# Five adaLN tiles from the mixer's output product to its first input products, conv LayerNorm steps scheduled earlier, conv chunks begun at once

## The chip, the cores and the metric

The kernel runs on one core of one Trainium2 chip. The metric is the device time of one execution in microseconds (us), the median of several runs. The core's engines run in parallel, each through its own instruction list in order: TensorE (PE, the matrix products), VectorE (DVE), ScalarE (ACT), GpSimd (POOL), and SyncE (SP), whose list here holds the DMA transfers.

## The reference

One block of a transformer on 256 tokens of width 2048, in float32. A conditioning vector is multiplied by a matrix (`w_ada`) and gives nine rows of shifts, scales and gates (adaLN). Then come a SwiGLU feed-forward (half weight), a mixer, and a second feed-forward, each with an RMS norm and a modulation before it and a gate after it. The mixer, which matters here:

```python
proj = jnp.einsum('bsd,de->bse', h, w_in)              # 2048 -> 5120 columns
q, k, v, conv_a, conv_g = jnp.split(proj, ...)
q = apply_rope(rms_norm(q, q_norm), cos, sin); k = apply_rope(rms_norm(k, k_norm), cos, sin)
attn = diff_attention(q, k, v, lam)                    # causal, two softmaxes, their difference
attn = (rms_norm(attn, subln) * (1.0 - lam_init)).reshape(B, S, ATTN_WIDTH)   # 1024 columns
u = conv_a * jax.nn.sigmoid(conv_g)                    # 1024 channels
u = causal_depthwise_conv(u, conv_w, conv_b)           # 31 taps along the tokens
u = jax.nn.silu(layer_norm(u, conv_ln_g, conv_ln_b))   # over the 1024 channels
merged = jnp.concatenate([attn, u], axis=-1)
return jnp.einsum('bse,ed->bsd', merged, w_out)        # 2048 -> 2048
```

## The kernel before

**Products.** float32 operands are split into a high part and a low part, and each product is three matmuls: high by high (L315), high of the activation by low of the weight (L316), low of the activation by high of the weight (L317), each 128x512. A weight tile is 128x2048 numbers (1 MB), fetched by SP into one of four `raw` buffers (`w_tile`). It is split in two halves: ACT makes `whi` (L294), DVE makes `wlo` (L296); each has four buffers, so two tiles are in flight. PE spends 24 matmuls on a tile, both 128-token tiles `t` included. Where a tile is held back or is the first of a stage, its halves lie in the general buffers and are called `blk`.

**adaLN.** `w_ada` is 144 further tiles of 1 MB. `ada(j)` fetches one into the same `raw` buffers (L180) and reduces it with the conditioning vector on DVE (L181, and a short read of the sum); each second one adds a bias (L185), and L223 makes a scale when a modulation is first asked for. `ada_share(r, limit)` lets a stage do r of these tiles on average until `limit` of them are done. They are spread over the stages that have room; 104 have to be there when the mixer ends.

**Mixer.** `w_in` is done in 10 chunks of 512 columns, `ci`, each with four weight tiles `pc`. Chunks 0 to 3 hold conv_a and conv_g (256 channels each), 4 to 9 are q, k, q, k, v, v. The first HOLD=3 chunks do their tile pc=0 together, while the norm's pieces still arrive (L425 to L430 are these pieces' modulation). After each tile's matmuls, work that was put off is called: `after_tiles(n, fn)` runs fn after n of the product's later steps, `tick` counts them. A finished chunk's results go into `pend`; they are taken up by `finish_mix` when the next chunk's first product has been issued. For chunks 0 to 3 that is `conv_chunk`: sigmoid and product (L777, L779), a transpose on PE and a copy (L788), the first of 31 taps by ACT (L769), and 60 taps on DVE (L771) put into the queue `bg`. `fill(n)` takes n taps from it after each tile; the table TAPS has n for each chunk.

**Output.** `w_out` has 16 tiles in order of `pc`, with n = 0, 1, 2 for each (12 tiles `i`), then n = 3 apart. pc = 0 and 1 need the attention half, pc = 2 and 3 the conv half (`mh[2]`, `mh[3]`). The first two tiles take TAPS_OUT taps; at i = 2 what is left of them is drained and `conv_ln` begins, in four steps: sums over channels (L937, L939, L941), mean by matmuls (L946), spreading over the partitions (L955), difference (L968) and squares, the sums again, the power on GpSimd (L977, L978), L955 once more, then scaling (L984), SiLU (L987) and the split into high (L990) and low (L991). Each step asks for the next by `after_tiles(1, ...)`.

**What sets the order.** Each instruction gets a priority in the order of the program's text; a scheduler writes each engine's list from priorities and dependencies before the run, and waits between the lists are semaphores. `tc.high_priority(offset=n)` moves what is written in its block n steps forward in that priority.

Of the kernel before, what the change touches and what calls it, by code (L numbers as in the profile page):

```python
# [35 lines left out]
UNITS = 3  # L36
PRE = 3
DVE_COLS = 2
AHEAD = 3
EXT = (1,) * 8 + (2,) * 4 + (3,) * 3  # L40
LOADS = [(0,), (1,), (2, 3), (4, 5), (6, 7)] + [(c,) for c in range(8, NCH)]
# [5 lines left out]
DUE = ((19, 8), (55, 16), (107, 24), (150, 32))  # L47


TAPS = (6, 6, 6, 6, 6, 6, 8, 6, 6, 6)  # L50
TAPS_OUT = 14
RMS_EPS = 1e-6
LN_EPS = 1e-5
LAM_INIT = 0.8 - 0.6 * float(np.exp(-0.3 * 0))
# [20 lines left out]
def block_kernel(ctx: ExitStack, tc: tile.TileContext, x_in, pos_in, w_ada, small, w_gu1, w_dn1,  # L75
# [56 lines left out]
    for i in range(4):  # L132
        pc = acc_tile()
# [13 lines left out]
    def fill(n):  # L147
        while n > 0 and bg:
            bg.popleft()()
            n -= 1  # L150

    def drain():
        while bg:
            bg.popleft()()
# [4 lines left out]
    def after_tiles(n, fn):  # L159
        later.append([n, fn])  # L160
# [116 lines left out]
    def w_tile(src, held=False, ks=(0, 4), small_raw=False):  # L277

        k0, n = ks[0], ks[1] - ks[0]
        src = src.rearrange("p (k n) -> p k n", k=4)  # L280
        if not small_raw:
            raw = rawp.tile([P, 4, 512], F32, tag="raw", name=nm("raw"))
            w_dma[0] = nc.sync.dma_start(out=raw[:, :n, :], in_=src[:, k0:k0 + n, :])
        views = {}
        for h in range(0, n, 2):
            m = min(2, n - h)
            if small_raw:
                part = blk([P, 2, 512])
                w_dma[0] = nc.sync.dma_start(out=part[:, :m, :], in_=src[:, k0 + h:k0 + h + m, :])
                rw = part[:, :m, :]  # L290
            else:
                rw = raw[:, h:h + m, :]
            hi = blk([P, 2, 512], F32R) if held else whp.tile([P, 2, 512], F32R, tag="whi", name=nm("whi"))
            nc.scalar.copy(out=hi[:, :m, :], in_=rw)  # L294
            lo = blk([P, 2, 512], F32R) if held else wlp.tile([P, 2, 512], F32R, tag="wlo", name=nm("wlo"))
            nc.vector.tensor_sub(out=lo[:, :m, :], in0=rw, in1=hi[:, :m, :].bitcast(F32))  # L296
            for j in range(m):
                views[k0 + h + j] = (hi[:, j, :], lo[:, j, :])
        return lambda j: views[j]
# [473 lines left out]
    def conv_chunk(cc, accs):  # L773
        us = []
        for t in range(NT):
            sg = tmp([P, 256])
            nc.scalar.activation(out=sg, in_=accs[t][:, 256:], func=AF.Sigmoid)  # L777
            u = tmp([P, 256])
            nc.vector.tensor_mul(out=u, in0=accs[t][:, :256], in1=sg)  # L779
            us.append(u)  # L780

        def rest():
            tp = tp_tile((P, 2, S))
            for t in range(NT):
                for i in range(2):
                    nc.tensor.transpose(tp[:, i, t * P:(t + 1) * P], us[t][:, i * P:(i + 1) * P], ident)
            uT[cc] = blk([P, 2, S])
            nc.scalar.copy(out=uT[cc], in_=tp)  # L788
            for j in reversed(range(CK)):
                for i in range(2):  # L790
                    bg.append(lambda i=i, j=j: conv_tap(cc, i, j))

        after_tiles(1, rest)
# [135 lines left out]
    def conv_ln():  # L929
        ones = tmp([P, 1])  # L930
        nc.gpsimd.memset(ones, 1.0 / 1024.0)

        def channel_mean(src):


            s4 = blk([P, 4, S])
            nc.vector.tensor_add(out=s4, in0=src[0], in1=src[1])  # L937
            s2 = tmp([P, 2, S])
            nc.vector.tensor_add(out=s2, in0=s4[:, :2, :], in1=s4[:, 2:, :])  # L939
            s1 = tmp([P, S])  # L940
            nc.vector.tensor_add(out=s1, in0=s2[:, 0, :], in1=s2[:, 1, :])  # L941

            def mean():
                m = tp_tile((P, NT))
                for t in range(NT):
                    nc.tensor.matmul(m[:, t:t + 1], s1[:, t * P:(t + 1) * P], ones, start=True, stop=True)  # L946
                return m

            return mean

        def spread(v):

            r = tp_tile((P, S))
            for t in range(NT):
                nc.tensor.transpose(r[:, t * P:(t + 1) * P], v[:, t:t + 1].to_broadcast([P, P]), ident)  # L955
            return r

        def stage1():
            summed = channel_mean(ytile)
            after_tiles(1, lambda: stage2(summed))  # L960

        def stage2(summed):
            mv = sm([P, NT], "rv")
            nc.vector.tensor_copy(out=mv, in_=summed())
            mean = spread(mv)
            sqs = []
            for b in range(2):
                nc.vector.tensor_sub(out=ytile[b], in0=ytile[b], in1=mean.unsqueeze(1).to_broadcast([P, 4, S]))  # L968
                q = blk([P, 4, S])
                nc.scalar.activation(out=q, in_=ytile[b], func=AF.Square)  # L970
                sqs.append(q)
            summed = channel_mean(sqs)
            after_tiles(1, lambda: stage3(summed))

        def stage3(summed):
            rv = sm([P, NT], "rv")
            nc.vector.tensor_scalar(out=rv, in0=summed(), scalar1=LN_EPS, scalar2=None, op0=ALU.add)  # L977
            nc.gpsimd.tensor_tensor(out=rv, in0=rv, in1=half[:, :NT], op=ALU.pow)  # L978
            after_tiles(1, lambda: stage4(rv))

        def stage4(rv):
            rs = spread(rv)
            for b in range(2):
                nc.vector.tensor_mul(out=ytile[b], in0=ytile[b], in1=rs.unsqueeze(1).to_broadcast([P, 4, S]))  # L984
                g0, b0 = _COLS["lng"][0] + 4 * b, _COLS["lnb"][0] + 4 * b
                for i in range(4):
                    nc.scalar.activation(out=ytile[b][:, i, :], in_=ytile[b][:, i, :], func=AF.Silu,  # L987
                                         scale=cst[:, g0 + i:g0 + i + 1], bias=cst[:, b0 + i:b0 + i + 1])
                mh[2 + b], ml[2 + b] = blk([P, 4, S], F32R), blk([P, 4, S], F32R)
                nc.scalar.copy(out=mh[2 + b], in_=ytile[b])  # L990
                nc.vector.tensor_sub(out=ml[2 + b], in0=ytile[b], in1=mh[2 + b].bitcast(F32))  # L991
                m_parts[2 + b] = NT

        stage1()


    kinds = [("q", 0), ("k", 0), ("q", 1), ("k", 1), ("v", 0), ("v", 1)]
    probs, avq = deque(), deque()

    def finish_mix(ci, accs):  # L1000
        if ci < 4:
            conv_chunk(ci, accs)
            return
        kind, g = kinds[ci - 4]
        if kind == "v":
            v_chunk(g, accs)
            avq.extend((g, qb, h_) for qb in range(2) for h_ in range(4))
        else:
            qk_chunk(kind, g, accs)
            if kind == "k":  # L1010
                if g == 0:
                    nc.scalar.activation(out=lsum, in_=lsum, func=AF.Exp)
                    nc.vector.tensor_sub(out=nlam, in0=lsum[:, 1:2], in1=lsum[:, 0:1])
                    nc.vector.tensor_scalar(out=nlam, in0=nlam, scalar1=-LAM_INIT, scalar2=None, op0=ALU.add)
                after_tiles(1, lambda: probs.extend((g, qb, h_) for qb in range(2) for h_ in range(4)))

    pend = []
# [6 lines left out]
    for ci in range(10):  # L1024
        p0 = 1 if ci < HOLD else 0
        accs = first[ci][2] if ci < HOLD else [acc_tile() for _ in range(NT)]
        for pc in range(p0, 4):
            if ci == 0 and pc < 3:
                for t in range(NT):
                    st.piece(pc + 1, t)  # L1030
            w = w_tile(w_in[ci, pc], ci == 0 and pc <= PRE)
            mm_tile(accs, w, act, 4 * pc, pc == 0, pc == 3)
            if pc == p0:
                while pend:
                    finish_mix(*pend.pop(0))
            fill(TAPS[ci])
            for _ in range(UNITS):
                if probs:
                    attn_probs(*probs.popleft())
                if avq:  # L1040
                    attn_av(*avq.popleft())
        pend.append((ci, accs))
    while pend:
        finish_mix(*pend.pop(0))

# [17 lines left out]
    accs = {}  # L1063
# [9 lines left out]
    for i, (n, pc) in enumerate([(n, pc) for pc in range(4) for n in range(3)]):  # L1073
        w = w_tile(w_out[n, pc])
        if i == 0:
            attention_step(len(probs) + len(avq))
        if i < 2:
            fill(TAPS_OUT)
        if i == 2:
            drain()  # L1080
            conv_ln()
            gbc = gate(80, 1.0)
        while m_parts[pc] < NT:
            later.pop(0)[1]()
        out_tile(n, pc, w, pc == 0, pc == 3)
        if i >= 5:
            ada_share(1.0, 104)
    flush()
    out_tile(3, 0, w_tile(w_out[3, 0]), True, False)
    held = [(pc, w_tile(w_out[3, pc], True)) for pc in range(1, 4)]  # L1090
# [90 lines left out]
```

## Time and profile before

| | |
|---|---|
| median of 3 runs | 1859.41 us (1859.16 to 1860.31) |
| the profiled execution | 1858.73 us |
| its span, first to last instruction | 1857.0 us, mean granted TensorE clock 0.994 |
| PE / DVE / ACT / POOL busy | 1823.5 / 1442.8 / 910.7 / 28.8 us |
| DMA | 495.91 MB, mean 267 GB/s |
| transfers on SP, from issue to landing (median) | adaLN tile 6.2 us, w_in tile 4.8 us, w_out tile 4.7 us |

Busy times are sums over the span. A timeline row has its start (us from the span's start), the duration, engine, line, operation, output<-inputs, and in brackets the engine's idle time before it with what ended that. A group row is followed by its count (x). Matmul rows overlap: one starts about 0.23 us after the last though its own duration is 0.39. A row of the windows gives the stretch, its length, then busy time and count for PE, PE's weight load, DVE, ACT and POOL, then granted clock, share of the DMA engines, GB/s.

### The profile page before, as it was taken

The page shows a single profiled execution, that of the slowest core. Times are in us where ns is not written, and L with a number is a line of the kernel's source. Part 1 is how long each engine was busy: PE and PEld are TensorE (multiplying, and loading weights), DVE is VectorE, ACT ScalarE, POOL GpSimd, SP SyncE. Part 2 cuts the span into 40 slices and gives each one's busy share as a digit, 9 for nine tenths or more (in the row PEclk, how much of TensorE's full clock was granted, in tenths as well). Part 3 has the DMA queues.
Part 4 walks back from the last instruction along what each step waited for, and adds up shares of the span by engine and source line. Part 5 has one row for each costly group of instructions (what it writes and reads, how often), then busy time and mean ns, then how long its engine had stood idle before and what let it go on. Part 6 is the DMA issues. An engine that isn't in the chain of part 4 may idle for free.

```text
span 1857.0 us, 21888 instructions
## 1 busy us (share of the span) xinstructions
PE 1823.5 (98%) x8247; PEld 1503.3 (81%) x8247; DVE 1442.8 (78%) x1922; ACT 910.7 (49%) x1378; POOL 28.8 (2%) x29
## 2 busy tenths in 40 slices
PE   6999999999999999999999899999999999999999
PEld 5788888888888887888888688888888888888887
DVE  7788869998888778789899968878877755544553
ACT  6553444444444443554776545664444444433332
POOL 0000000000000000000110000000000000000000
PEclk8999999999999999999999899999999999999999
DMA  9888968889989898645444667888777755556552
GB/s 384 336 318 302 344 253 317 336 297 342 328 327 367 341 355 331 241 178 181 159 159 159 249 227 276 338 321 333 269 279 281 281 182 194 191 206 213 196 212 79
DMA packets 72730, 495.91 MB, mean 267 GB/s; under 512 B 8193, under 2 KB 8625, under 8 KB 15153
## 3 DMA queue, kind: packets, MB, share of 16 engines
q1 hardware_dynamic: 72624, 494.53, 71.6%
q8 instruction: 64, 1.05, 0.2%
q14 instruction: 42, 0.34, 0.0%
HBM read 492.37 MB, written 2.12 MB: 266 GB/s over the span
## 4 chain that ended last, share of the span: by engine, by line
PE 91%; DVE 4%; DMA 2%; ACT 1%; issue 1%; POOL 0%; SPq 0%; POOLq 0%; DVEq 0%; ACTq 0%
PE acc L316 30%; PE acc L317 30%; PE acc L315 29%; DMA blk<-in_w_gu_dram 1%; DVE wlo L296 1%; DVE blk L771 1%; PE tp L588 1%; DMA raw<-in_w_ada_dram 1%; PE acc L863 1%; PE tp L377 1%; ACT whi L294 0%; DVE raw L181 0%; ACT tmp L825 0%; POOL rv L978 0%; DVE blk L923 0%
## 5 line engine op out<-in xcount | busy, mean ns | idle before, releaser
L294 ACT CAST whi<-raw 128x1024 fp32r<-128x1024 f32 (+1 forms) x605 | 628.0, 1046 | 751.7 <-PE acc L317 605.8
L296 DVE TENSOR_TENSOR wlo<-raw,whi 128x1024 fp32r<-128x1024 f32 (+1 forms) x605 | 724.7, 1211 | 319.8 <-ACT whi L294 318.7
L315 PE MATMUL acc<-whi,blk 128*128 128x512 f32 x2448 | 957.4, 393 | 10.8 <-ACT blk L990 4.8
L316 PE MATMUL acc<-wlo,blk 128*128 128x512 f32 x2448 | 956.9, 391 | 2.5 <-DVE wlo L296 2.5
L317 PE MATMUL acc<-whi,blk 128*128 128x512 f32 x2448 | 956.1, 391 | 1.1 <-DVE blk L991 1.1
L315 PEld LDWEIGHTS acc<-whi,blk 128*128 128x128 f32 x2448 | 460.9, 188 | 107.3 <-ACT blk L990 5.1
L316 PEld LDWEIGHTS acc<-wlo,blk 128*128 128x128 f32 x2448 | 461.3, 188 | 99.3 <-DVE wlo L296 5.6
L317 PEld LDWEIGHTS acc<-whi,blk 128*128 128x128 f32 x2448 | 460.5, 188 | 98.8 <-DVE blk L991 1.8
L181 DVE CUSTOM_DVE_ANT_0 raw<-raw,c_bc 128x2048 f32<-128x2048 f32 x142 | 324.2, 2284 | 10.1 <-DMA raw<-in_w_ada_dram 9.9
L771 DVE SCALAR_TENSOR_TENSOR blk<-blk,cst,blk 128x255 f32<-128x255 f32 (+14 forms) x240 | 97.6, 458 | 0.0
L468 ACT COPY blk<-acc 128x512 f32<-128x512 f32 x88 | 49.8, 591 | 60.3 <-PE acc L317 58.4
L580 DVE TENSOR_TENSOR blk<-acc,blk 128x512 f32<-128x512 f32 x88 | 56.7, 682 | 0.1
L315 PE MATMUL acc<-blk,blk 128*128 128x512 f32 x112 | 43.9, 393 | 0.0
L317 PE MATMUL acc<-blk,blk 128*128 128x512 f32 x112 | 43.8, 391 | 0.0
L316 PE MATMUL acc<-blk,blk 128*128 128x512 f32 x112 | 43.6, 389 | 0.0
L296 DVE TENSOR_TENSOR blk<-raw,blk 128x1024 fp32r<-128x1024 f32 x28 | 33.8, 1220 | 2.1 <-ACT blk L294 1.9
L582 DVE TENSOR_TENSOR blk<-blk 128x256 f32<-128x256 f32 x88 | 33.3, 417 | 0.5 <-ACT blk L581 0.5
L581 ACT ACTIVATE blk<-blk 128x256 f32<-128x256 f32 x88 | 32.2, 411 | 1.4 <-DVE blk L580 1.4
L294 ACT CAST blk<-raw 128x1024 fp32r<-128x1024 f32 x28 | 28.9, 1050 | 7.7 <-DMA raw<-in_w_dn_dram 6.5
L334 DVE TENSOR_TENSOR blk<-tp,blk 128x512 fp32r<-128x512 f32 x44 | 29.9, 684 | 1.8 <-ACT blk L333 1.8
L343 ACT ACTIVATE tmp<-xall 128x512 f32<-128x512 f32 x22 | 13.8, 632 | 30.1 <-DVE xall L641 16.7
L333 ACT CAST blk<-tp 128x512 fp32r<-128x512 f32 x44 | 25.3, 580 | 2.4 <-PE tp L588 2.4
(149 smaller groups left out, 665.9 us busy)
## 6 DMA issues: line engine op xcount, KB each, us to landing
raw<-in_w_gu_dram SPq DMA_DIRECT2D x161, 1024.0 KB, 5.3
raw<-in_w_ada_dram SPq DMA_DIRECT2D x142, 1024.0 KB, 6.2
raw<-in_w_dn_dram SPq DMA_DIRECT2D x88, 1024.0 KB, 4.9
raw<-in_w_in_dram SPq DMA_DIRECT2D x40, 1024.0 KB, 4.8
raw<-in_w_out_dram SPq DMA_DIRECT2D x16, 1024.0 KB, 4.7
raw<-in_w_gu_dram SPq DMA_DIRECT2D x8, 768.0 KB, 5.5
blk<-in_w_gu_dram SPq DMA_DIRECT2D x10, 512.0 KB, 13.9
blk<-gate_line SPq DMA_DIRECT2D x6, 512.0 KB, 6.9
```

The source lines that it names most:

```text
L181: nc.vector.tensor_tensor_reduce(out=raw, in0=raw, in1=c_bc, scale=1.0, scalar=0.0, op0=ALU.mult, op1=ALU.add, accum_out=ada_cols[g][:, j ...
L294: nc.scalar.copy(out=hi[:, :m, :], in_=rw)
L296: nc.vector.tensor_sub(out=lo[:, :m, :], in0=rw, in1=hi[:, :m, :].bitcast(F32))
L315: nc.tensor.matmul(acc, ah, wh, start=start, stop=False)
L316: nc.tensor.matmul(acc, ah, wl, start=False, stop=False)
L317: return nc.tensor.matmul(acc, al, wh, start=False, stop=stop)
L334: nc.vector.tensor_sub(out=lo, in0=tp, in1=hi.bitcast(F32))
L468: last_part[0] = nc.scalar.copy(out=parts[c][:, t, :], in_=accs[t])
L580: nc.vector.tensor_add(out=p[:, t, :], in0=accs[t], in1=p[:, t, :])
L581: nc.scalar.activation(out=p[:, t, :256], in_=p[:, t, :256], func=AF.Silu)
L582: nc.vector.tensor_mul(out=p[:, t, 256:], in0=p[:, t, :256], in1=p[:, t, 256:])
L771: nc.vector.scalar_tensor_tensor(out=y[:, d:], in0=u, scalar=w, in1=y[:, d:], op0=ALU.mult, op1=ALU.add)
```

## The change

Four edits. The last five adaLN tiles before 104 (99 to 103) are asked for at the mixer's start (ci = 0 from pc = 2, all of ci = 1), not in the output product from i = 5. The four steps of `conv_ln` run under a priority 150 steps ahead. A conv chunk is taken up when its own last tile is issued, not after the next chunk's first. TAPS takes 8 and 7 rather than 6 at chunks 1 and 2, and TAPS_OUT 12 rather than 14. No operation is added or removed.

```diff
+SOONER = 150
...
-TAPS = (6, 6, 6, 6, 6, 6, 8, 6, 6, 6)
-TAPS_OUT = 14
+TAPS = (6, 8, 7, 6, 6, 6, 8, 6, 6, 6)
+TAPS_OUT = 12
...
+        def sooner(stage, arg):
+
+            with tc.high_priority(offset=SOONER):
+                stage(arg)
+
         def stage1():
             summed = channel_mean(ytile)
-            after_tiles(1, lambda: stage2(summed))
+            after_tiles(1, lambda: sooner(stage2, summed))
...
-            after_tiles(1, lambda: stage3(summed))
+            after_tiles(1, lambda: sooner(stage3, summed))
...
-            after_tiles(1, lambda: stage4(rv))
+            after_tiles(1, lambda: sooner(stage4, rv))
...
-        stage1()
+        with tc.high_priority(offset=SOONER):
+            stage1()
...
     def finish_mix(ci, accs):
-        if ci < 4:
-            conv_chunk(ci, accs)
-            return
...
             w = w_tile(w_in[ci, pc], ci == 0 and pc <= PRE)
+            if ci == 1 or ci == 0 and pc > 1:
+                ada_share(1.0, 104)
             mm_tile(accs, w, act, 4 * pc, pc == 0, pc == 3)
             if pc == p0:
                 while pend:
                     finish_mix(*pend.pop(0))
+            if pc == 3 and ci < 4:
+                conv_chunk(ci, accs)
             fill(TAPS[ci])
...
-        pend.append((ci, accs))
+        if ci >= 4:
+            pend.append((ci, accs))
...
         out_tile(n, pc, w, pc == 0, pc == 3)
-        if i >= 5:
-            ada_share(1.0, 104)
```

Lines after the first edit are one higher in the changed kernel, and 6 or 7 higher from `conv_ln`'s second step on (L181 becomes L182, L296 L297, L771 L772, L779 L780, L955 L956, L977 L983, L984 L990, L990 L996, L991 L997).

**SP at the mixer's start.** The rows are the transfers of `w_in` tiles into `raw`; before:

```order
L283 DMA raw_6117<-in_w_in_dram 128x2048
L283 DMA raw_6179<-in_w_in_dram 128x2048
L283 DMA raw_6213<-in_w_in_dram 128x2048
L283 DMA raw_6255<-in_w_in_dram 128x2048
L283 DMA raw_6302<-in_w_in_dram 128x2048
```

and now:

```order
L284 DMA raw_6117<-in_w_in_dram 128x2048
L181 DMA raw_6127<-in_w_ada_dram 128x2048
L284 DMA raw_6183<-in_w_in_dram 128x2048
L181 DMA raw_6193<-in_w_ada_dram 128x2048
L284 DMA raw_6228<-in_w_in_dram 128x2048
L181 DMA raw_6238<-in_w_ada_dram 128x2048
L284 DMA raw_6281<-in_w_in_dram 128x2048
L181 DMA raw_6291<-in_w_ada_dram 128x2048
L284 DMA raw_6326<-in_w_in_dram 128x2048
L181 DMA raw_6336<-in_w_ada_dram 128x2048
```

From the sixth weight tile on, five adaLN tiles alternate with weights; their five rows in the output product are gone.

**DVE around the weight tile ci = 2, pc = 1.** Its two halves are wlo_6346 and wlo_6350 before, wlo_6384 and wlo_6388 now; acc_5911 is chunk 0's result, acc_5923 chunk 1's. Before:

```order
L779 TENSOR_TENSOR tmp_6253<-acc_5912,tmp_6251 128x256
L296 TENSOR_TENSOR wlo_6346<-raw_6342,whi_6344 128x1024
L296 TENSOR_TENSOR wlo_6350<-raw_6342,whi_6348 128x1024
L771 SCALAR_TENSOR_TENSOR blk_5899<-blk_6294,cst,blk_5899 128x255 x2
L771 SCALAR_TENSOR_TENSOR blk_5899<-blk_6294,cst,blk_5899 128x254 x2
```

and now, with the rows between the two halves left out but for the last seven:

```order
L780 TENSOR_TENSOR tmp_6366<-acc_5923,tmp_6364 128x256
L772 SCALAR_TENSOR_TENSOR blk_5899<-blk_6271,cst,blk_5899 128x249
L780 TENSOR_TENSOR tmp_6370<-acc_5924,tmp_6368 128x256
L772 SCALAR_TENSOR_TENSOR blk_5899<-blk_6271,cst,blk_5899 128x248 x2
L772 SCALAR_TENSOR_TENSOR blk_5899<-blk_6271,cst,blk_5899 128x247 x2
L772 SCALAR_TENSOR_TENSOR blk_5899<-blk_6271,cst,blk_5899 128x246 x2
L772 SCALAR_TENSOR_TENSOR blk_5899<-blk_6271,cst,blk_5899 128x245 x2
L297 TENSOR_TENSOR wlo_6388<-raw_6380,whi_6386 128x1024
L772 SCALAR_TENSOR_TENSOR blk_5899<-blk_6271,cst,blk_5899 128x244 x2
```

The second half's wlo now stands behind 22 taps of chunk 0 (13 of them ahead of the first row shown) and chunk 1's two products.

**DVE in the conv LayerNorm, from the power's input to the last split.** Before:

```order
L977 TENSOR_SCALAR rv_8565<-tp_8566 128x2
L181 ISA raw_8735,ada_5698<-raw_8735,c_bc 128x2048
L181 ISA ada_5698 128x1
L984 TENSOR_TENSOR blk_5899<-blk_5899,tp_8605 128x1024
L984 TENSOR_TENSOR blk_5900<-blk_5900,tp_8605 128x1024
L296 TENSOR_TENSOR wlo_8709<-raw_8701,whi_8707 128x1024
L185 TENSOR_TENSOR ada_5698<-ada_5698,cst 128x2
L181 ISA raw_8773,ada_5698<-raw_8773,c_bc 128x2048
L181 ISA ada_5698 128x1
L223 SCALAR_TENSOR_TENSOR scales<-ada_5698,cst 128x1 x2
L991 TENSOR_TENSOR blk_8614<-blk_5899,blk_8613 128x1024
```

and now:

```order
L983 TENSOR_SCALAR rv_8583<-tp_8584 128x2
L990 TENSOR_TENSOR blk_5899<-blk_5899,tp_8623 128x1024
L990 TENSOR_TENSOR blk_5900<-blk_5900,tp_8623 128x1024
L297 TENSOR_TENSOR wlo_8686<-raw_8678,whi_8684 128x1024
L997 TENSOR_TENSOR blk_8632<-blk_5899,blk_8631 128x1024
```

The two adaLN reductions are gone from between the steps; so are the two before them in this stage (one between L939 and L941) and the one after.

On PE, the last L955 before is followed at once by the matmuls on blk_8613, the conv half's high part:

```order
L955 MATMUL tp_8605<-cst,rv_8565 128x128 x2
L315 MATMUL acc_8348<-whi_8666,blk_8613 128x512
L316 MATMUL acc_8348<-wlo_8668,blk_8613 128x512
L317 MATMUL acc_8348<-whi_8666,blk_8614 128x512
L315 MATMUL acc_8349<-whi_8666,blk_8613 128x512
```

Now a whole tile on the attention half (blk_8458, blk_8459) follows, of which the first rows are

```order
L956 MATMUL tp_8623<-cst,rv_8583 128x128 x2
L316 MATMUL acc_8493<-whi_8646,blk_8458 128x512
L317 MATMUL acc_8493<-wlo_8648,blk_8458 128x512
L318 MATMUL acc_8493<-whi_8646,blk_8459 128x512
L316 MATMUL acc_8494<-whi_8646,blk_8458 128x512
```

and 24 matmuls stand before the first that reads the conv half (blk_8631):

```order
L318 MATMUL acc_8494<-whi_8650,blk_8459 128x512
L316 MATMUL acc_8379<-whi_8680,blk_8631 128x512
L317 MATMUL acc_8379<-wlo_8682,blk_8631 128x512
L316 MATMUL acc_8380<-whi_8680,blk_8631 128x512
L317 MATMUL acc_8380<-wlo_8682,blk_8631 128x512
L318 MATMUL acc_8379<-whi_8680,blk_8632 128x512
```

Between the last spreading and its first dependent stands one weight tile, where there was none.

## The prediction

> **What bounds the kernel now.** I read the page first: busy shares, then the chain that ended last.
>
> ```profile
> span 1857.0 us, 21888 instructions
> PE 1823.5 (98%) x8247; PEld 1503.3 (81%) x8247; DVE 1442.8 (78%) x1922; ACT 910.7 (49%) x1378; POOL 28.8 (2%) x29
> PE 91%; DVE 4%; DMA 2%; ACT 1%; issue 1%; POOL 0%; SPq 0%; POOLq 0%; DVEq 0%; ACTq 0%
> ```
>
> PE is busy in 1823.5 of 1857.0 us. The change adds no matmul, so only PE's 33.5 idle us and its time at a reduced clock can be won, whatever the edits do on other engines. Next the list of waits, for PE alone (total, times, longest):
>
> ```profile
> PE acc L315 <- ACT blk L990: 4.8, 1, 4.8
> PE acc L316 <- DVE wlo L296: 2.5, 5, 0.8
> PE tp L955 <- POOL rv L978: 2.1, 1, 2.1
> PE tp L946 <- DVE tmp L941: 1.1, 1, 1.1
> PE acc L317 <- DVE blk L991: 1.1, 1, 1.1
> ```
>
> Four of the five belong to the conv LayerNorm (L937 to L991), 9.1 us in all. The timeline of PE there shows what comes on top:
>
> ```profile
> 1054.53 0.43 PE L955 MATMUL tp<-cst,rv 128*128 128x128 f32 x2 [2.06 <-POOL rv L978]
> 1059.81 0.80 PE L315 MATMUL acc<-whi,blk 128*128 128x512 f32 x1 [4.85 <-ACT blk L990]
> 1062.10 0.79 PE L317 MATMUL acc<-whi,blk 128*128 128x512 f32 x1 [1.07 <-DVE blk L991]
> 1062.69 0.63 PE L315 MATMUL acc<-whi,blk 128*128 128x512 f32 x1
> 1063.12 0.63 PE L316 MATMUL acc<-wlo,blk 128*128 128x512 f32 x1
> ...
> 1065.68 0.48 PE L316 MATMUL acc<-wlo,blk 128*128 128x512 f32 x1
> 1066.00 0.39 PE L317 MATMUL acc<-whi,blk 128*128 128x512 f32 x1
> 1066.23 0.39 PE L315 MATMUL acc<-whi,blk 128*128 128x512 f32 x1
> ```
>
> From 1066.00 on, one matmul follows another in 0.23 us; from 1062.69 on, in 0.43 us: PE runs at half clock after the two gaps. From 1059.81 to 1066.00 there are 11 matmul steps in 6.19 us, where 11 x 0.227 = 2.49 us would do: 3.70 us lost, the wait of 1.07 included. The stage thus loses 1.14 + 2.06 + 4.85 + 3.70 = 11.75 us. (The L946 wait is 1.14 in the timeline, 1.1 above.) This is the pot. The last view is the windows, which tell whether VectorE has room where the work is moved to:
>
> ```profile
> 800.00:840.00 40.00, 40.00 (x182) 33.12 (x181) 31.85 (x60) 18.84 (x25) 0.00 (x0) 1.00 0.50 181
> 840.00:880.00 40.00, 40.00 (x181) 33.08 (x181) 40.00 (x79) 18.54 (x41) 0.85 (x1) 1.00 0.53 187
> 1040.00:1080.00 40.00, 32.02 (x132) 25.39 (x131) 30.41 (x34) 19.79 (x24) 2.67 (x1) 0.87 0.80 293
> ```
>
> The fourth number is VectorE's busy time: 8.15 us free in the first window, none in the second; in the third PE is busy for 32.02 us at a granted clock of 0.87.
>
> **The LayerNorm: what is won.** The next rows are VectorE's, ScalarE's and GpSimd's around the same place.
>
> ```profile
> 1034.75 2.28 DVE L181 CUSTOM_DVE_ANT_0 raw<-raw,c_bc 128x2048 f32<-128x2048 f32 x1
> 1036.96 0.41 DVE L941 TENSOR_TENSOR tmp<-tmp 128x256 f32<-128x256 f32 x1
> 1051.57 0.15 DVE L977 TENSOR_SCALAR rv<-tp 128x2 f32<-128x2 f32 x1
> 1051.64 2.28 DVE L181 CUSTOM_DVE_ANT_0 raw<-raw,c_bc 128x2048 f32<-128x2048 f32 x1
> 1058.48 2.28 DVE L181 CUSTOM_DVE_ANT_0 raw<-raw,c_bc 128x2048 f32<-128x2048 f32 x1
> 1060.83 1.22 DVE L991 TENSOR_TENSOR blk<-blk,blk 128x1024 fp32r<-128x1024 f32 x1
> 1058.73 1.03 ACT L990 CAST blk<-blk 128x1024 fp32r<-128x1024 f32 x1
> 757.66 0.55 POOL L142 TENSOR_TENSOR rstd<-rstd,half 128x1 f32<-128x1 f32 x1 [744.09 <-DVE rstd L141]
> 1051.81 2.67 POOL L978 TENSOR_TENSOR rv<-rv,half 128x2 f32<-128x2 f32 x1 [29.57 <-DVE rv L977]
> ```
>
> *First mean (L946).* An adaLN reduction of 2.28 us runs between L939 and L941. In the new order a wlo of 1.2 us stands there instead. Walking VectorE's new order with these durations, L941 ends some 0.2 us after PE arrives: 1.14 becomes 0.2.
>
> *The power (L978) and L955.* L978 raises 128x2 numbers and takes 2.67 us; L142 is the same operation and took 0.55 us at 757.66. The difference: L978 starts 0.17 us after a reduction on VectorE and ends 0.56 us after that one's end (1053.92), as if it had waited for it. The new order has no reduction behind L977; the next VectorE instruction, L984, waits for L955 itself. I take 0.55, the row that has nothing beside it, and PE's wait goes from 2.06 to 0.3; the other end is 2.67 again, with the wait of 2.1 kept. The Trainium skill ("SBUF — State Buffer", section "SBUF: two separate sides") states that GpSimd and a VectorE instruction with two SBUF inputs take a shared port pair as an exclusive lock, and the later one blocks until the first ends; the two rows agree with it, but they show one such meeting only.
>
> *The scaled result (L984 to L990).* L955 starts at 1054.53 and the first matmul on the conv half at 1059.81: 5.28 us of L984, SiLU and L990, in which PE has nothing. In the new order 24 matmuls on the attention half stand behind the last L955: 24 x 0.227 = 5.44 us, and L955 itself. The wait of 4.85 becomes 0; this step's cover is thin, 0.2 to 0.5 us.
>
> *The low part (L991).* It starts at 1060.83, held by the reduction of 1058.48, though its input L990 ended at 1059.76. Without the reduction it ends at about 1061.0, 1.2 us after L990, and the first two products on a conv tile now both take the high part: wait 0 instead of 1.07.
>
> *The clock.* Without gaps of 2.06 and 4.85 us I expect no half clock: 3.70 goes to 0. If the pow stays slow, one gap of 2.1 us remains, and no row shows what a lone gap of that length does; the bounds are 0 and the 2.63 us (3.70 - 1.07) that the two gaps cost. The Trainium skill ("TensorE: Matmul & The Clock Gate", section "Part 1: The HAM clock gate") has the clock fall after an idle window of some 3.4 us; by it a lone 2.1 us costs nothing.
>
> Won: 11.75 - 0.2 - 0.3 = 11.25 us.
>
> **The five adaLN tiles, now at the mixer's start.** Each is a transfer of 1 MB on SP's queue, one L181 of 2.28 us (with its read some 2.3), and a share of L185 and L223 of 0.15 to 0.2 us: 11.5 to 12 us of VectorE work between 770 and 811. The room there, VectorE's idle stretches, in brackets:
>
> ```profile
> 784.90 2.36 DVE L296 TENSOR_TENSOR wlo<-raw,whi 128x1024 fp32r<-128x1024 f32 x2 [3.17 <-ACT whi L294]
> 789.70 0.69 DVE L430 TENSOR_TENSOR blk<-tmp,blk 128x512 fp32r<-128x512 f32 x1 [1.15 <-ACT blk L429]
> 804.34 0.42 DVE L779 TENSOR_TENSOR tmp<-acc,tmp 128x256 f32<-128x256 f32 x1 [4.50 <-ACT tmp L777]
> 805.92 1.23 DVE L296 TENSOR_TENSOR wlo<-raw,whi 128x1024 fp32r<-128x1024 f32 x1 [1.16 <-ACT whi L294]
> 808.63 1.23 DVE L296 TENSOR_TENSOR wlo<-raw,whi 128x1024 fp32r<-128x1024 f32 x1 [1.16 <-ACT whi L294]
> ```
>
> 11.1 us in these five rows: it fits, barely, if each reduction falls where VectorE idles. On SP each transfer now alternates with a weight tile and takes its buffer, so the next weight waits for a reduction. Where L430 or a wlo stands behind a reduction, PE can be late. Ends: 0, and one whole reduction uncovered, 2.3. I take 0.5, since in my walk the worst pieces arrive within half a microsecond of their use. At their old place the reductions cost only what is counted above.
>
> **Taps and channel sums at once.** For each of the four conv chunks conv_chunk runs one product earlier, and TAPS gives 8 and 7 to chunks 1 and 2. The number of taps stays. In the new order, 22 taps and two L779 stand between two halves of the weight tile c=2, pc=1:
>
> ```profile
> 811.23 0.58 ACT L788 COPY blk<-tp 128x512 f32<-128x512 f32 x1
> 811.84 1.10 ACT L769 ACTIVATE blk<-blk,cst 128x256 f32<-128x256 f32 x2
> 811.36 1.23 DVE L296 TENSOR_TENSOR wlo<-raw,whi 128x1024 fp32r<-128x1024 f32 x1 [1.50 <-ACT whi L294]
> 812.50 4.09 DVE L771 SCALAR_TENSOR_TENSOR blk<-blk,cst,blk 128x255 f32<-128x255 f32 x10
> 818.95 0.39 PE L316 MATMUL acc<-wlo,blk 128*128 128x512 f32 x1
> ```
>
> Before, both halves' wlo come first: the second, of 811.36, ends at 812.59, 6.37 us ahead of its use by PE at 818.95. In the new order the second half's wlo stands behind the taps. These can start when L769 has its input, which the earlier call brings forward: by the walk at about 811.1, just before the 811.84 of now. One tap takes at most 4.09 / 10 = 0.41 us, an L779 about as much (0.42 in the rows above): 24 x 0.41 = 9.8 us; a little less, 9.3, since such rows overlap by some hundredths. With 1.2 us for the wlo itself it is ready at 821.6, against 818.95 + 0.5 (the loss above): PE waits some 2 us. The next wlo stands behind seven more taps (2.8 us) and is some 1.3 us late; from there on the taps between two wlo are as many as before and VectorE gains the lead back in its 8 us of free time in that window. I take 3.3. Ends: 0 (taps start earlier, or the free time absorbs them), and 5 (the walk is 1.7 us optimistic on L769).
>
> After that, in the attention part, the waits of L316 for a wlo (2.5 us in five) can go or grow: VectorE does some 5 us less just before the worst of them and more ahead of that. I take +0.3; ends -2.5 and +2.
>
> **Sum.** -11.25 + 0.5 + 3.3 + 0.3 = -7.15 us, against the profiled execution's 1858.73 us (its span of 1857.0 and 1.73 around it): 1851.6. The median of the runs, 1859.41, is 0.68 above that execution, so I say 1852.3.
>
> **Rivals.**
>
> *The start eats the gain (no change that can be seen).* The early reductions and the taps both take their upper ends: 2.3 + 5 + 2 = 9.3 of 11.25 us, which gives 1859.41 - 1.95 = 1857.5. For it: VectorE is busy 40.00 of 40 us at 840 to 880, so a lead lost before is not regained there. Against: 8 us are free between 800 and 840, and 11.1 in the idle stretches before.
>
> *Nothing is lost at the start.* All of the early work hides: 1859.41 - 11.25 = 1848.2, and 1847.5 if attention's waits shrink as well. For it: a lead of 6.37 us at the place in question. Against: 22 taps, 9 us, are longer than the lead.
>
> *The power stays slow.* L978's 2.67 us are its own: L955 waits 2.1 rather than 0.3 (+1.8), and the clock falls in part of such cases (0 to 2.6): 1854.1 to 1856.7. Against it are 0.55 us for the same operation, and the end half a microsecond behind the reduction's.
>
> *Slower: VectorE's backlog meets in one place.* If the transfers land late, so that the 11.5 us of reductions hide nothing, they stand ahead of the taps' 9.3 us: 20.8 us of work in front of a wlo with a lead of 6.37, so PE waits 14.4 us in one gap, and the clock falls as after the 4.85-us gap (2.6): 17.0 - 11.25 = +5.8, that is 1865.2. It decides from a wait of about 8.7 us there (with 2.6 for the clock, that makes 11.25). Against it: 11.1 us of idle time in the rows above would have to be of no use, and SP issues these five transfers in turn with weights, some 5 us of matmuls apart.
>
> *The change doesn't do what it says:* the priority would leave the LayerNorm where it is. The written order excludes that for the reductions and for the 24 matmuls; I give it nothing of its own.
>
> **How the numbers follow.** Chances: the sum as walked, 1850 to 1854, 0.40; nothing lost at the start 0.15; slow power 0.13; the start eats the gain 0.22; backlog 0.10. A change under 0.2% (3.7 us) can't be told from none here: faster means below 1855.7, slower above 1863.1. Faster: 0.40 + 0.15, most of the slow power (0.10), and a small part of the fourth case (0.04) = 0.69. Slower: the backlog's worst part, 0.09. The rest, 0.22, is the same. The range for 8 in 10 goes from 1847.7 (nothing lost at the start) to 1858.5 (the start eats the gain); it leaves out the backlog and a part of the fourth case.
>
> **What would show it.** In the profile after: no wait of L315 for L990 and none of L317 for L991; matmuls at 0.23 us throughout 1040 to 1080, granted clock 1.00 there; L978 (with its new line number) at 0.55 rather than 2.67 us. The loss at the start would show as new waits of L316 for wlo between 815 and 830, 2 to 4 us in all, and small ones by L430 or wlo between 775 and 805. I am wrong if PE waits more than 5 us between 770 and 830, if a half clock shows up in the w_out stage, or if L955 still waits 2 us; the first two would move the result by more than the last.

## The result, and the profile after

The changed kernel takes 1851.03 us (median of 5 runs, 1848.81 to 1851.34) against 1859.41 before: a ratio of 0.9948 (0.9934 to 0.9961). In a later series beside other variants it took 1849.90 against 1859.46, 0.9951 (0.9939 to 0.9964). The profiled execution took 1848.81 us, its span 1847.0.

Page of the changed kernel, its span, busy times and the chain that ended last:

```profile
span 1847.0 us, 21889 instructions
PE 1820.2 (99%) x8247; PEld 1501.6 (81%) x8247; DVE 1442.0 (78%) x1922; ACT 911.9 (49%) x1378; POOL 26.5 (1%) x29
PE 93%; DVE 3%; ACT 1%; DMA 1%; issue 1%; POOL 0%; SPq 0%; POOLq 0%; DVEq 0%; ACTq 0%
```

PE's idle time went from 33.5 to 26.8 us (1847.0 - 1820.2), and PE is busy 3.3 us less with the same matmuls. Before, its granted clock was 0.50 from 62.34 to 65.75 and from 1055.62 to 1065.86 us, where matmuls follow each other in 0.43 rather than 0.23 us; now it is at full clock at both places, and only the half clock of the start lasts longer, until 23.54 rather than 21.38 us. Its list of waits, the rows that answer to those of before:

```profile
PE acc L317 <- DVE wlo L297: 4.6, 5, 2.0
PE acc L903 <- ACT blk L847: 0.7, 1, 0.7
PE acc L316 <- ACT blk L996: 0.3, 1, 0.3
```

The waits for the power, for the sum and for the low part are gone from the list, and the 4.8 us for the high part is 0.3 (L996 is L990 of before). What is longer is the wait for a wlo: 4.6 instead of 2.5, the longest 2.0. The windows show the same two places:

```profile
800.00:840.00 40.00, 37.28 (x167) 30.28 (x166) 38.76 (x74) 18.99 (x26) 0.00 (x0) 1.00 0.62 224
840.00:880.00 40.00, 40.00 (x182) 33.12 (x181) 40.00 (x76) 17.52 (x30) 0.00 (x0) 1.00 0.58 203
1040.00:1080.00 40.00, 39.60 (x176) 31.80 (x175) 27.77 (x28) 26.54 (x32) 0.69 (x1) 1.00 0.59 215
```

In the last one PE is busy 39.60 us instead of 32.02, at full clock. In the first it is busy 37.28 instead of 40.00, and VectorE 38.76 instead of 31.85: the moved work filled the free time there, and more.

To see what each stretch gained I lay matching instructions side by side: the same transpose ahead of the mixer, the first matmul of a step in the attention part, another at its end, and one behind the output product. First the changed kernel, then the kernel before (start, duration):

```profile
766.67 0.33 PE L378 MATMUL tp<-cst,tmp 128*128 128x128 f32 x1 [0.21 <-DVE tmp L370]
914.76 0.35 PE L864 MATMUL acc<-blk,blk 128*128 128x128 f32 x1
1014.27 0.38 PE L903 MATMUL acc<-blk,blk 128*128 128x128 f32 x1 [0.68 <-ACT blk L847]
1104.02 0.41 PE L378 MATMUL tp<-cst,tmp 128*128 128x128 f32 x2 [0.55 <-DVE tmp L370]
```

```profile
767.98 0.33 PE L377 MATMUL tp<-cst,tmp 128*128 128x128 f32 x1 [0.21 <-DVE tmp L369]
912.69 0.35 PE L863 MATMUL acc<-blk,blk 128*128 128x128 f32 x1
1013.22 0.38 PE L902 MATMUL acc<-blk,blk 128*128 128x128 f32 x1 [0.47 <-ACT blk L846]
1113.89 0.30 PE L377 MATMUL tp<-cst,tmp 128*128 128x128 f32 x1 [0.56 <-DVE tmp L369]
```

The lead is 1.31 us at the first, -2.07 at the second, -1.05 at the third, 9.87 at the last. So the first chunks lost 3.38 us, the attention part won 1.02, and the LayerNorm with the output product won 10.92. The 1.31 us at the start lie ahead of all that was changed and belong to these two executions; the change itself is worth 8.56 us between the profiles (9.87 less 1.31).

### The profile page after: what moved, and what is told of

Its sections match the earlier page's. It is cut to its first block, busy times and chain, and to the rows that moved or that the text cites. A ratio compares the mean times of both kernels' runs of the same rounds, so it can differ in the third digit from the quotient of the medians.

```text
span 1847.0 us, 21889 instructions
## 1 busy us (share of the span) xinstructions
PE 1820.2 (99%) x8247; PEld 1501.6 (81%) x8247; DVE 1442.0 (78%) x1922; ACT 911.9 (49%) x1378; POOL 26.5 (1%) x29
## 3 DMA queue, kind: packets, MB, share of 16 engines
q8 instruction: 64, 1.05, 0.2%
## 4 chain that ended last, share of the span: by engine, by line
PE 93%; DVE 3%; ACT 1%; DMA 1%; issue 1%; POOL 0%; SPq 0%; POOLq 0%; DVEq 0%; ACTq 0%
PE acc L317 30%; PE acc L318 30%; PE acc L316 30%; DVE blk L772 1%; PE tp L589 1%; DVE wlo L297 1%; DMA blk<-in_w_gu_dram 1%; PE acc L864 1%; PE tp L378 1%; DMA blk<-in_w_ada_dram 1%; ACT whi L295 0%; PE acc L903 0%; DVE raw L182 0%; ACT blk L469 0%; PE tp L813 0%
## 5 line engine op out<-in xcount | busy, mean ns | idle before, releaser
L297 DVE TENSOR_TENSOR wlo<-raw,whi 128x1024 fp32r<-128x1024 f32 (+1 forms) x605 | 725.7, 1212 | 318.3 <-ACT whi L295 316.9
L316 PE MATMUL acc<-whi,blk 128*128 128x512 f32 x2448 | 957.0, 393 | 5.8 <-ACT blk L387 2.2
L316 PEld LDWEIGHTS acc<-whi,blk 128*128 128x128 f32 x2448 | 460.5, 188 | 102.0 <-ACT whi L295 2.8
L182 DVE CUSTOM_DVE_ANT_0 raw<-raw,c_bc 128x2048 f32<-128x2048 f32 x142 | 324.4, 2285 | 5.3 <-DMA raw<-in_w_ada_dram 4.8
L772 DVE SCALAR_TENSOR_TENSOR blk<-blk,cst,blk 128x255 f32<-128x255 f32 (+17 forms) x240 | 97.5, 463 | 0.5 <-ACT blk L770 0.5
L316 PE MATMUL acc<-blk,blk 128*128 128x512 f32 x112 | 43.7, 393 | 0.0
L297 DVE TENSOR_TENSOR blk<-raw,blk 128x1024 fp32r<-128x1024 f32 x28 | 33.7, 1220 | 1.8 <-ACT blk L295 1.8
```

The source lines that it names most:

```text
L182: nc.vector.tensor_tensor_reduce(out=raw, in0=raw, in1=c_bc, scale=1.0, scalar=0.0, op0=ALU.mult, op1=ALU.add, accum_out=ada_cols[g][:, j ...
L316: nc.tensor.matmul(acc, ah, wh, start=start, stop=False)
L772: nc.vector.scalar_tensor_tensor(out=y[:, d:], in0=u, scalar=w, in1=y[:, d:], op0=ALU.mult, op1=ALU.add)
```

## The experiments

Two theories. A: the move of the five reductions out of the LayerNorm brings the gain, and the taps that now come early cost part of it back. B: the priority, which is named for this, brings the LayerNorm forward, and the move mostly adds work at the mixer's start. Runs of one series share a chip and the runs of before (medians 1859.31, 1859.46, 1859.29). The last three columns are the us won over the profile of before between the four marks above: in the first chunks, in the attention part, and in the LayerNorm with the output product. They leave out the start of the span, which no edit touches and which alone differs by 2.5 us between these profiles (the first mark lies between 766.36 and 768.84 us).

| kernel | median, us | ratio to before | first chunks | attention | LayerNorm, output |
|---|---|---|---|---|---|
| the change, first series | 1851.03 | 0.9948 (0.9934 to 0.9961) | -3.4 | 1.0 | 10.9 |
| move alone | 1847.84 | 0.9941 (0.9928 to 0.9953) | 0.0 | -0.3 | 9.8 |
| move and priority | 1850.07 | 0.9949 (0.9936 to 0.9961) | -0.1 | -0.3 | 9.7 |
| priority, call at once, new taps | 1856.77 | 0.999 (0.9981 to 0.9999) | -2.2 | 1.0 | 2.5 |
| priority alone | 1857.72 | 0.999 (0.9981 to 0.9999) | 0.0 | 0.0 | 1.4 |
| the change with the old taps | 1853.01 | 0.9966 (0.9953 to 0.9978) | -0.7 | -4.3 | 10.9 |
| the change again | 1849.90 | 0.9951 (0.9939 to 0.9964) | -4.0 | 1.0 | 10.9 |
| move, priority, other taps | 1846.09 | 0.9928 (0.9915 to 0.9942) | 0.0 | 0.7 | 10.9 |
| the change, sums added behind the power (SCALAR_TENSOR_TENSOR) | 1855.31 | 0.9977 (0.9968 to 0.9987) | -3.9 | 1.0 | 6.5 |
| the same with TENSOR_TENSOR, one execution | 1855.77 | | -3.4 | 1.0 | 5.5 |
| move, other taps, no priority | 1846.62 | 0.9931 (0.9917 to 0.9944) | -0.1 | 0.8 | 11.0 |
| call at once and new taps alone | 1859.42 | 1.0 (0.9991 to 1.0009) | -2.2 | 1.0 | 0.5 |

**The move alone.** The kernel before with

```diff
+            if ci == 1 or ci == 0 and pc > 1:
+                ada_share(1.0, 104)
...
-        if i >= 5:
-            ada_share(1.0, 104)
```

> The kernel before with the adaLN move alone: old taps, old call of conv_chunk, no priority. Theory A (the move of the five reductions clears the LayerNorm; the earlier taps cost 3 us at chunk 2): the whole late gain without that cost, 1847.5 to 1849.5 us, no wait of L955 on the power, none at the weight tile c=2 pc=1. Theory B (the priority is what brings the LayerNorm forward; the move alone mostly adds work at the mixer's start): 1856 us or more, with L990 still waited for.

Measured 1847.84 us: as much as the complete change. The intervals of the two overlap; in the profiles, without the start, it is 9.5 us against 8.56, since nothing is lost in the first chunks. From its list of waits:

```profile
PE acc L316 <- DVE wlo L296: 2.2, 4, 0.8
PE tp L946 <- DVE tmp L941: 1.1, 1, 1.1
PE acc L315 <- ACT blk L990: 0.3, 1, 0.3
```

The waits for L990, the power and L991 are gone without any priority, and no wlo is late by more than 0.8. Only the first sum still comes 1.1 us late, though no reduction stands ahead of it any more. In this kernel's order, too, 24 matmuls on the attention half stand behind the last L955. Theory B falls.

**Move and priority.** The change with `finish_mix`, `pend`, TAPS and TAPS_OUT as before.

> The changed kernel with the old call of conv_chunk and the old TAPS and TAPS_OUT: move and priority remain. Theory A: the 2.9 us of waits at 820 and 824 us vanish and the late gain stays: 1847.5 to 1849.5 us, the same as with the move alone within 1 us. Theory B: also about 1848, but then clearly faster than the move alone. Rival C (the new taps are needed so that the last taps end in time): L947 waits 2 us or more for the channel sums, 1850 to 1852.

1850.07 us. The waits at 820 us are gone (no wlo is waited for by more than 0.8), as theory A has it, but the median is 2.2 us above the move alone, where I had said 1. The profiled executions of the two are equal in span (1847.2 and 1847.0) and show the same waits, and each stretch is equal within 0.2 us; the intervals of the two ratios overlap. Rival C had something: L947 waits 1.2 us for the first sum, with the priority as without. What makes the 2.2 us between the medians isn't settled.

**Without the move.** The change with `ada_share(1.0, 104)` back at i >= 5.

> The changed kernel with the five adaLN tiles back in the output product. Theory A: the last spreading again has no attention tile behind it, so the wait of about 5 us for L990 and the half clock come back, and the loss at chunk 2 stays (22 taps still stand ahead of the second half's wlo): 1858 to 1863 us. Theory B: 1850 to 1852, as with the change.

1856.77 us, just below the range; theory B's 1850 to 1852 is far. Timeline of PE, the rows with long waits:

```profile
819.48 0.50 PE L317 MATMUL acc<-wlo,blk 128*128 128x512 f32 x1 [0.85 <-DVE wlo L297]
823.29 0.50 PE L317 MATMUL acc<-wlo,blk 128*128 128x512 f32 x1 [0.79 <-DVE wlo L297]
1051.14 0.43 PE L956 MATMUL tp<-cst,rv 128*128 128x128 f32 x2 [0.71 <-POOL rv L984]
1058.95 0.79 PE L316 MATMUL acc<-whi,blk 128*128 128x512 f32 x1 [6.44 <-ACT blk L996]
```

The gap ahead of the conv half is back, at 6.44 us even longer. At 819 the first wait is 0.85 instead of 1.96 us: of the loss at chunk 2, 1.1 us come from the reductions that stand ahead there, the rest from the taps.

**The priority alone.** The kernel before with `with tc.high_priority(offset=SOONER)` around the four steps.

> The kernel before with the priority alone. Theory A: reductions only change places among the LayerNorm's steps; two now stand ahead of L991: 1857 to 1862 us, with a wait of about 5 us for L990. Theory B: 1848 to 1850.

1857.72 us, with the same 6.44 us for L996 and 0.7 for the power. A: a shift among the steps, no cover.

**Old taps.** The change with

```diff
-TAPS = (6, 8, 7, 6, 6, 6, 8, 6, 6, 6)
-TAPS_OUT = 12
+TAPS = (6, 6, 6, 6, 6, 6, 8, 6, 6, 6)
+TAPS_OUT = 14
```

> The changed kernel with the old TAPS and TAPS_OUT; move, priority and the call at once stay. Now 15 taps instead of 22 stand ahead of the second half's wlo at chunk 2. Theory A (seven taps of 0.39 us are the wait of 2.0 us): the wlo comes 2.8 us sooner, the waits at 820 and 824 us go, 1847.5 to 1849.5 us. Rival (the late call of the taps was not the cause, but the reductions ahead of them): the waits stay at 2 to 3 us.

1853.01 us: slower than the change, not faster. The waits at 820 do go, as A says (no gap longer than 0.1 us is left there). But the attention part loses 4.3 us, where the change wins 1.0:

```profile
937.14 0.50 PE L317 MATMUL acc<-wlo,blk 128*128 128x512 f32 x1 [0.51 <-DVE wlo L297]
946.03 0.50 PE L317 MATMUL acc<-wlo,blk 128*128 128x512 f32 x1 [1.94 <-DVE wlo L297]
948.08 0.63 PE L316 MATMUL acc<-whi,blk 128*128 128x512 f32 x1
948.51 0.63 PE L317 MATMUL acc<-wlo,blk 128*128 128x512 f32 x1
```

The taps not done early come late: in this kernel's order 14 of them stand between two wlo ahead of 931 us, 8 before. That this sets VectorE back until 946 us is likely, but no run tests it. The wait of 1.94 us is followed by matmuls at 0.43 us apart, a half clock. My theory had the right price at chunk 2 (16 taps stand there, 6 fewer, and the wlo comes 2.6 us sooner) and missed where the taps would go.

**The change again.**

> The changed kernel once more, beside the others on one chip. 1849 to 1851.5 us; the profile has waits of L317 for wlo of 2.0 and 0.9 us at 820 and 824.

1849.90 us. One thing differs from the first profile at this place; PE's timeline:

```profile
822.76 0.63 PE L316 MATMUL acc<-whi,blk 128*128 128x512 f32 x1
823.19 0.63 PE L317 MATMUL acc<-wlo,blk 128*128 128x512 f32 x1
823.62 0.63 PE L318 MATMUL acc<-whi,blk 128*128 128x512 f32 x1
...
825.75 0.41 PE L317 MATMUL acc<-wlo,blk 128*128 128x512 f32 x1
826.00 0.40 PE L318 MATMUL acc<-whi,blk 128*128 128x512 f32 x1
```

After the wait of 1.94 us at 820 this execution ran at half clock until 825.75; the first profile of the same kernel, after its wait of 1.96 us, did not. The second wait, at 824, is then swallowed, since PE is slower.

**A better version.** Move and priority, the old call of `conv_chunk`, and

```diff
-TAPS = (6, 6, 6, 6, 6, 6, 8, 6, 6, 6)
-TAPS_OUT = 14
+TAPS = (6, 6, 7, 7, 7, 6, 8, 6, 6, 6)
+TAPS_OUT = 12
```

> Move and priority, the old call of conv_chunk, and TAPS 7 at chunks 2, 3 and 4 with TAPS_OUT 12, so that one tap more, not eight, stands between two halves where the lead is small, and the last taps end before the LayerNorm's first sum. Theory A: no wait at 820, L947 waits 0.2 rather than 1.1 us: 1846 to 1848.5 us, 0.5 to 1.5 below the move alone. Rival (VectorE is full from 840 to 880, so the extra taps there make a wlo late): 1849 to 1852.

1846.09 us, the fastest of all and below the range's middle. It has no wait for the first sum, and for wlo 1.8 us in three waits, all ahead of the mixer: none at 820 and none in the attention part. One tap more after each tile of chunks 2, 3 and 4 is enough to let the last tap end at 1014.41 us, where it ends at 1027.42 with the move alone.

**Work behind the power.** The change with

```diff
-            nc.gpsimd.tensor_tensor(out=rv, in0=rv, in1=half[:, :NT], op=ALU.pow)
+            r1 = sm([P, NT], "rv")
+            nc.gpsimd.tensor_tensor(out=r1, in0=rv, in1=half[:, :NT], op=ALU.pow)
+            d = tmp([P, 2, S])
+            with tc.high_priority(offset=1000):
+                for b in range(3):
+                    nc.vector.scalar_tensor_tensor(out=d, in0=ytile[0][:, :2, :], scalar=rv[:, :1], ...)
```

> The changed kernel with added VectorE work (three sums of 128x512 that nothing uses) right behind the power's input, in the order 0.7, 0.7, a wlo of 1.2, 0.7 us. Theory A (GpSimd's power waits for the one VectorE instruction that runs when it arrives, then takes 0.55): the power takes 1.1 to 1.3 us instead of 0.69. Rival 1 (it waits until VectorE is idle): 3.3 to 4 us. Rival 2 (the operation is slow by itself): 0.69. The scaling L995 starts behind the added work in any case, some 2 us later, so L316 waits for the conv half's high part by some 2 us: 1851 to 1854 us in all.

VectorE's first two added sums and GpSimd's power:

```profile
1047.93 1.57 DVE L989 SCALAR_TENSOR_TENSOR tmp<-blk,rv,blk 128x512 f32<-128x512 f32 x2
1047.97 0.69 POOL L985 TENSOR_TENSOR rv<-rv,half 128x2 f32<-128x2 f32 x1 [24.04 <-DVE rv L983]
```

The power took 0.69 us beside a SCALAR_TENSOR_TENSOR of 0.78 that started 0.04 us earlier: by that, rival 2. But that rival then has no answer for 2.67 us before and 1.60 us in the two kernels with a wlo there (the priority alone, and the change without the move). The total, 1855.31, is above the range: L316 waits 3.2 us instead of 2 and a half clock follows.

**The same with plain sums.** `nc.vector.tensor_tensor(out=d, in0=ytile[0] half, in1=rv[:, :1] broadcast, op=ALU.add)` three times.

> As with the added work behind the power's input, but with plain sums of two tensors (TENSOR_TENSOR, 128x512, 0.7 us each), the kind of a wlo. Theory A, narrowed by the last run (a plain two-tensor operation holds the power back, a SCALAR_TENSOR_TENSOR doesn't): the power starts 0.1 to 0.2 us into the first sum and ends some 0.55 us after that one's end: 1.0 to 1.2 us. Rival (only the long operations of 1.2 us and more, the wlo and the reduction, hold it back): 0.69.

VectorE's first two sums and GpSimd's power:

```profile
1047.68 1.42 DVE L989 TENSOR_TENSOR tmp<-blk,rv 128x512 f32<-128x512 f32 x2
1047.73 1.20 POOL L985 TENSOR_TENSOR rv<-rv,half 128x2 f32<-128x2 f32 x1 [24.07 <-DVE rv L983]
```

The two sums take 1.42 us, 0.7 each, so the first ends at about 1048.4; the power ends at 1048.93, some 0.55 us later. As theory A, narrowed, has it. The second sum, in its turn, isn't held back by the power that is still running (1.42 us for the two). With the rows of the other kernels there is a series:

| VectorE beside the power | power, us | ends after the VectorE instruction |
|---|---|---|
| nothing (the change, move alone and others) | 0.69 to 0.70 | |
| SCALAR_TENSOR_TENSOR, 0.78 us | 0.69 | |
| TENSOR_TENSOR, 0.7 us | 1.20 | 0.55 |
| wlo (TENSOR_TENSOR), 1.22 us | 1.60 | 0.54 |
| adaLN reduction, 2.28 us (before; the call at once and new taps alone) | 2.67 | 0.56 |

**The better version without priority.** The same with the `with` line taken out.

> The best version so far without the priority: move, old call, new taps. Theory A (with the reductions gone and the taps early, the steps stand in nearly the same order without it): L946 waits up to 1.1 us, as in the move alone, since both splits of L923 stand ahead of the first sum; everything else alike: 1846 to 1847.5 us. Theory B (the priority carries part of the gain): 1848 us or more.

1846.62 us, within the interval of the one with it. The L946 wait I had said up to 1.1 for isn't in its list of waits. The medians differ by half a microsecond, less than the intervals, and the stretches by 0.1: on top of the move no worth of the priority can be told from nothing.

**The call at once and the new taps alone.**

> The kernel before with only the call at once and the new TAPS. Theory A: the LayerNorm's order is the old one with all four waits and the half clock, and chunk 2's waits of 2 to 3 us come on top, less some 0.5 us for waits in the attention part that go: 1860 to 1862.5 us, slower than before. Rival (earlier taps free VectorE for the LayerNorm): 1856 or less.

1859.42 us, ratio 1.0 (0.9991 to 1.0009): no change that can be seen, and below the range I gave. The LayerNorm has three of its four waits (4.8, 2.1 and 1.1 us in the list), and two waits at chunk 2 come on top, but each of these is only 0.8 us without the reductions ahead of them, and the attention part's waits go. The first sum's wait is gone, though a reduction stands ahead of L942 as before:

```profile
1033.85 2.29 DVE L182 CUSTOM_DVE_ANT_0 raw<-raw,c_bc 128x2048 f32<-128x2048 f32 x1
1036.06 0.42 DVE L942 TENSOR_TENSOR tmp<-tmp 128x256 f32<-128x256 f32 x1
1036.63 0.58 PE L947 MATMUL tp<-tmp,tmp 128*128 128x1 f32 x4
```

## Why the prediction was right

It said 1852.3 us (1847.7 to 1858.5); 1851.03 was measured. Term by term, from the profiles:

- *The LayerNorm, -11.25.* Measured -10.92. L990 leaves 0.31 us where I said 0, the low part some 0.2, both from the thin cover that the text named; and the gap for the power is 0 where I had put 0.3. No half clock between 1040 and 1080.
- *The first sum, 0.94 of these.* L947 starts 0.16 us late (0.2 said), but that is luck, since the reason given is wrong. The text put the wait down to the reduction between L939 and L941. With the move alone that reduction is gone and L946 still waits 1.1 us; with the call at once and the new taps alone it is there and L947 waits for nothing. What differs is where VectorE's last tap ends: at 1028.37 us before and 1027.42 with the move alone, at 1011.49 in the change and 1010.73 with the call and taps alone. (In the change with the old taps it ends at 1027.96, but there PE itself comes 4.3 us later out of the attention part than with the move alone, and doesn't wait.) The better version, which differs from move and priority in the numbers of taps alone, has no such wait where that kernel has 1.2 us. So of the 10.92 us some 9.8 come from the move, and some 1.1 from taps that end earlier.
- *The power.* Right in kind: it is held back by the VectorE instruction beside it, and the move takes that away; this is now shown by the series above. The size was off by 0.14: 0.69, not 0.55, because the row I took had one column and this one two. GpSimd's rows of after show the trend with nothing beside them:

```profile
1017.65 1.01 POOL L143 TENSOR_TENSOR rs<-rs,half 128x4 f32<-128x4 f32 x1 [6.02 <-DVE rs L142]
1046.23 0.69 POOL L984 TENSOR_TENSOR rv<-rv,half 128x2 f32<-128x2 f32 x1 [24.03 <-DVE rv L983]
```

- *The five reductions at the mixer's start, +0.5, and the taps, +3.3.* Measured 3.38 together, against 3.8. The waits are where the walk had put them. VectorE and PE in the profile after:

```profile
809.84 5.32 DVE L772 SCALAR_TENSOR_TENSOR blk<-blk,cst,blk 128x255 f32<-128x255 f32 x13 [0.51 <-ACT blk L770]
816.13 3.18 DVE L772 SCALAR_TENSOR_TENSOR blk<-blk,cst,blk 128x248 f32<-128x248 f32 x8
819.22 1.22 DVE L297 TENSOR_TENSOR wlo<-raw,whi 128x1024 fp32r<-128x1024 f32 x1
820.50 0.50 PE L317 MATMUL acc<-wlo,blk 128*128 128x512 f32 x1 [1.96 <-DVE wlo L297]
824.30 0.50 PE L317 MATMUL acc<-wlo,blk 128*128 128x512 f32 x1 [0.75 <-DVE wlo L297]
```

The taps start at 809.84, and with the 1.31 us that this execution is ahead, that is the 811.1 of the walk. The waits of 1.96 and 0.75 answer to "some 2" and 1.3. What the text did not see is that the two terms act together: the reductions alone cost nothing (0.0 with the move alone), call and taps alone 2.2 us, both 3.4. Without the reductions ahead of the taps the first wait is 0.85.

- *The attention part, +0.3.* Wrong in sign: -1.02, inside the ends given. With the change's own taps the worst wlo before, at 944.60, is no longer late.
- *The sum, -7.15*, stands against 8.56 us between the profiles without the 1.31 at the start, and 8.4 between the medians. The 1.4 us between sum and profiles are the attention part's 1.3, the start's 0.4, less 0.3 in the LayerNorm.

Of the rivals, "the start eats the gain" and "the power stays slow" did not come. "Nothing is lost at the start" is what the move alone does (1847.84, beside the rival's 1848.2). On the priority the text was cautious, and it had no term; alone it brings some 1.6 us, on top of the move nothing that these runs can tell. The range's lower end, 1847.7, comes out of no sum: the rival that it is named after gives 1848.2, or 1847.5 with the attention part's waits.

The reading of the clock fell. For a lone gap of 2 us, should the power stay slow, the text gave 0 to 2.6 us; its sum has no term for the clock at the gap of some 2 us at chunk 2. It cited the Trainium skill ("TensorE: Matmul & The Clock Gate", section "Part 1: The HAM clock gate"), by which only an idle window of some 3.4 us costs anything. Here a lone wait of 1.94 us was followed by half clock in one profile of the changed kernel, and one of 1.96 us was not in the other; in the kernel with the old taps half clock followed one of 1.94 us. The measurement decides: such a gap can cost up to 8 matmul steps of 0.2 us, 1.6 us, on top of itself.

The traces also show when. The granted clock in them changes in pieces of 3.41 us. The rows give a piece, its length, PE's busy time, granted clock, share of the DMA engines and GB/s; first two pieces of the kernel before, then of the changed kernel's second profile, then of its first:

```profile
58.93:62.34 3.41, 1.50 (x5) 1.00 0.98 408
62.34:65.75 3.41, 3.41 (x9) 0.50 0.64 231
818.96:822.37 3.41, 1.50 (x7) 1.00 0.23 36
822.37:825.78 3.41, 3.41 (x10) 0.50 0.66 271
818.84:822.25 3.41, 1.75 (x8) 1.00 0.26 41
822.25:825.67 3.42, 2.67 (x12) 1.00 0.63 266
```

In all 13 profiles, between 25 and 1800 us, the clock fell from full to half 13 times. PE had been busy for at most 1.72 us of the piece before each time, and for 1.75 us or more of every piece at full clock behind which it did not fall. What counts in these traces is thus how much of a wait falls into one piece, and where the pieces lie differs from execution to execution. The rows of the kernel before, with a wait of 1.62 us at 60.31 and one of 0.53 at 61.57, could be read ahead of the result; the prediction says that no row shows what a lone gap of 2.1 us does, and passed these over, the nearest there are.

Half clock after such waits may be why the runs of the changed kernel stand in two groups (1848.8 to 1849.1 and 1851.0 to 1851.3). The runs list only a mean granted clock, 0.996 and 0.998 in the faster group and 0.994 to 0.995 in the slower. That fits but doesn't say where the clock fell, so it stays open.

## What to carry to other kernels

When the critical engine waits in a chain of small steps, look first for long optional work that sits between them on the helper engines; moving it to where these idle gave nearly all of the gain here, and reordering by priority next to none. Count what the moved work stands in front of at its new place: 22 taps ahead of one weight half, with reductions ahead of them, cost 3.4 us, a third of what had been won. Test each cause alone, even when the number comes out: the first sum's wait went as forecast and for another reason. Queued work that is taken out of one place comes up in another, so shift it by small amounts to each place that has lead, and look at the waits of the whole stage afterwards.

## What the runs showed of the hardware

A GpSimd power of 128x2 numbers that starts during a VectorE TENSOR_TENSOR whose two inputs lie in SBUF, or during an adaLN reduction, ends 0.54 to 0.56 us after that instruction, however long it is (0.7, 1.22 or 2.28 us). A SCALAR_TENSOR_TENSOR with two tensors in SBUF didn't hold it back in the one such meeting here (0.69 us, as with nothing beside it); beside a row of taps, which are of that kind, a power of 128x4 took 1.15 rather than 1.01 us. For the first kind the runs agree with the Trainium skill ("SBUF — State Buffer", section "SBUF: two separate sides"), which lets a VectorE instruction with two SBUF inputs lock GpSimd out until it ends; the second kind is not as it states. PE's half clock came after single waits of less than 2 us, in some executions of a kernel and not in others, when PE had been busy for at most 1.72 of a piece of 3.41 us.
